# Shared buffers for the up and down stage, a paired token order in the out projection, and operand addresses equal modulo 512 bytes

## The chip, the core and the metric

The kernel runs on one core of a Trainium2 chip. Its time is the device time of one execution in microseconds (us); where several runs are given, their median. TensorE (PE) multiplies matrices into PSUM, VectorE (DVE) and ScalarE (ACT) do elementwise work, GpSimd (POOL) some more of it, and SyncE (SP) issues the DMAs, in the order in which they are written for it. A weight load of PE is listed as PEld.

## The reference

One encoder block on x of 1024 tokens by 1024 channels, in float32:

```
h = rmsnorm(x) * norm_mix_g ; proj = h @ w_in            # 1024 x 2048
u, q, k, v = split(proj, 512 columns each)
a = per group of 128 channels: (centred mean over 2, 4, 8 or 16 tokens - u) @ w_pool, times pool_scale
b = neighbourhood attention over a 16 x 64 grid, 8 heads of 64, window 8 x 16, with a relative bias
x = x + concat(a, b) @ w_out                             # 1024 x 1024
h = rmsnorm(x) * norm_mlp_g
x = x + square(relu(h @ w_up)) @ w_down                  # 1024 x 4096, 4096 x 1024
out = rmsnorm(x) * final_g
```

## The kernel before

**Split operands.** Each float32 operand is cut into a rounded high part and the remainder, both of type float32r: `split` is an ACT cast (line 90) and a DVE subtraction (line 91). `three` (lines 133, 135, 137) multiplies high by high, high by low and low by high into one PSUM bank of 128 x 512, so every product of a 128-deep slice is three wide matmuls.

**Stages.** First come the projections (operands hh and hl against weights wh, wl, wvh, wvl), the pool groups and the attention, with the projections as filler between the attention tiles (`filler`, `pump`). `out_pools` multiplies the pooled half of the mixed channels (`mixed`, split into `msp` tiles) with the first half of w_out (`woh`, `wol`) and stores the sum with x in DRAM (`ad`). The out stage (lines 748 to 768) takes the eight token tiles of 128 in order 0 to 7: it adds the attention half of w_out to the loaded `acc`, stores it as x2, normalises it into `hn2`, and one tile later `h2t` transposes it (line 724).

**Up and down stage.** Both MLP products use a seven-product scheme for 2 x 2 blocks. The token axis is cut in halves (tiles 0 to 3 and 4 to 7), the channels in halves too, and four operands `ops` are blocks while 5, 6, 7 and others are sums of blocks; tile t of one half and tile t + 4 of the other enter the same sum. In `h2t` of before, tiles 0 to 3 fill ops 1 and 2 and keep raw copies `b11r`, `b21r`; tiles 4 to 7 make t1 (ops 5), `t2r` and a raw copy `b22r`. Ops 6, 7, 3 and 4 are made after the last tile from these raw copies (`t_split`, `t_sum`, lines 832 to 846). The up stage runs over 16 pairs of blocks of w_up, seven products each in the order 1 5 6 2 7 3 4, each of 12 wide matmuls; `cut` makes the w_up operand `s` some five products ahead, `evacuate` empties PSUM, `stored` writes the results and their sums to DRAM (`us`), and `lazy` holds the sums back. Two pairs of blocks (`EARLY`) have their products 1 and 2 done while the last tiles are made ready.

Then all buffers of the up stage are closed, new ones opened, and the down stage runs its seven products over 16 blocks each: `load_d` brings two blocks of w_down and `us`, `cut_pair` splits two operands into `st` (four blocks ahead), `four` multiplies for four token tiles into four banks, `after` empties them. In the last product the last five blocks (`STAGGERED`) are held back and then done token tile by token tile, so that the closing norm of one tile runs under the matmuls of the next.

**Buffers.** Tiles come from pools with a fixed number of slots; an instruction that fills a slot waits until its former content was used up. Up to the early products the order of the work is the planner's (it simulates the program), behind them (`manual_schedule`) it is the order written. `t4` tiles of 4 KB per partition serve x, weights, mixed, msp, acc, hn2 and the early w_up operands alike, 16 slots of 4160 bytes, since the wide `t4w` shares them. `t16` has four slots for hh, hl and later w_out.

Of the kernel before, what the change touches and what calls it, by code (L numbers as in the profile page):

```python
# [30 lines left out]
NPAIR = 16  # L31
EARLY = 2


@with_exitstack
def block_kernel(ctx, tc, x, norm_mix_g, w_in, w_pool, pool_scale, rpb, w_out,
# [32 lines left out]
    def t16(name):  # L69
        return k16.tile([P, 4096], F32R, tag="k16", name=name)  # L70
# [109 lines left out]
    hh = quads([t16("hh0"), t16("hh1")])  # L180
    hl = quads([t16("hl0"), t16("hl1")])
    with ExitStack() as pv:
# [24 lines left out]
        for i in range(4):  # L207
            raw = t4("wvraw").rearrange("p (c n) -> p c n", c=2)
# [191 lines left out]
    with ExitStack() as pt_:  # L400
# [157 lines left out]
        def wo_half(i):  # L558

            wos[i] = t16("woh"), t16("wol")  # L560
            for c in range(4):
                wo_chunk(i, c)
# [15 lines left out]
        def m_split(src, th, pool, tag, eng=None):  # L578

            m = pool.tile([P, 1024], F32R, tag=tag, name="msp").rearrange("p (l t) -> p l t", l=2)  # L580
            split(m[:, 0, :], m[:, 1, :], src[:, th * HALF:(th + 1) * HALF], lo_eng=eng)
            return m

# [3 lines left out]
        def out_pools():  # L587
            wos[1] = t16("woh"), t16("wol")
            for th in range(2):
                for tt in range(4 * th, 4 * th + 4):  # L590
# [10 lines left out]
                    if th == 0:  # L601
                        later.append(lambda g=tt: ma[1].append(m_split(mixed[g], 1, qk, "qk")))
                    elif tt < 7:
                        later.append(lambda h=tt - 4: mb[0].append(m_split(bs[h], 0, k4, "k4")))
# [3 lines left out]
        def filler():  # L608

            finish = None  # L610
            for o in order[1:]:
# [11 lines left out]
                if o == "q3":  # L623
                    later.extend(lambda g=g: ma[0].append(m_split(mixed[g], 0, k4, "k4")) for g in range(4))
# [53 lines left out]
        mb[0].append(m_split(bs[3], 0, k4, "k4"))  # L678
# [7 lines left out]
    hbs = ExitStack()  # L686
    hb = hbs.enter_context(tc.tile_pool(name="hb", bufs=3, reuse_waits="tile"))
    ue = hbs.enter_context(tc.tile_pool(name="ue", bufs=EARLY, reuse_waits="tile"))
    hrs = ExitStack()
    hrp = hrs.enter_context(tc.tile_pool(name="hr", bufs=4, reuse_waits="tile"))  # L690

    def t_op(pool):
        return pool.tile([P, 2, 4, HALF], F32R, tag="h", name="hop")


    ops = {i: t_op(hb) for i in (1, 2, 5)}
    b11r, b21r, t2r, b22r = [hrp.tile([P, 4, HALF], F32, tag="hr", name="hr") for _ in range(4)]

    def load_early(b):
        raw = t4("uraw").rearrange("p (c n) -> p c n", c=NC8)  # L700
        nc.sync.dma_start(out=raw, in_=w_up[:, 2 * b * P:(2 * b + 1) * P]
                          .rearrange("(c p) n -> p c n", p=P))
        out = []
# [11 lines left out]
    def h2t(hn, tt):  # L715
# [3 lines left out]
        pts = []  # L719
        for g in range(2):  # L720
            pt = bank("ST"[g])
            for k in range(4):
                c = 4 * g + k
                nc.tensor.transpose(pt[:, k * P:(k + 1) * P], hn[:, c * P:(c + 1) * P], ident)
            pts.append(pt.rearrange("p (k t) -> p k t", k=4))
        if th == 0:
            for pv, raw, o in zip(pts, (b11r, b21r), (ops[1], ops[2])):
                nc.scalar.copy(out=raw[:, :, tsl], in_=pv)
                split(o[:, 0, :, tsl], o[:, 1, :, tsl], raw[:, :, tsl])
        else:  # L730
            t1 = t2("t1").rearrange("p (k t) -> p k t", k=4)
            nc.vector.tensor_tensor(out=t1, in0=pts[0], in1=b11r[:, :, tsl], op=ALU.subtract)
            nc.vector.tensor_tensor(out=t2r[:, :, tsl], in0=pts[1], in1=t1, op=ALU.subtract)
            nc.scalar.copy(out=b22r[:, :, tsl], in_=pts[1])
            split(ops[5][:, 0, :, tsl], ops[5][:, 1, :, tsl], t1)
# [3 lines left out]
    acc = []  # L739
    hn = None  # L740
    early = []

    def load_acc(tt):
        a = t4("acc")
        nc.sync.dma_start(out=a, in_=ad[tt * P:(tt + 1) * P, :])
        acc.append(a)
# [3 lines left out]
    for th in range(2):  # L750
        for tt in range(4 * th, 4 * th + 4):
            a = acc[tt]
            if tt + 2 < NC8:
                load_acc(tt + 2)
            for nh in range(2):
                nsl = slice(nh * HALF, (nh + 1) * HALF)
                ps = bank(("pp", "O")[tt % 2])
                run(out_half(mb[th], wos[1], tt, nh, ps))
                nc.vector.tensor_tensor(out=a[:, nsl], in0=ps, in1=a[:, nsl], op=ALU.add)
# [389 lines left out]
```

## Time and profile before

| | |
|---|---|
| median of three runs | 1043.28 us (1040.67 to 1043.54) |
| profiled execution | 1040.96 us, its span 1039.2 us |
| PE busy | 988.6 us, 95% of the span |
| DVE, ACT, POOL busy | 63%, 52%, 16% of the span |
| mean granted PE clock | 0.98 of full speed |
| DMA | 159.14 MB, mean 153 GB/s |

Busy shares are averages over stages with different limits. PE's matmuls overlap, so the duration of one is longer than the distance between two starts. Times inside the rows below count from the start of the span.

### The profile page before, as it was taken

The page shows a single profiled execution, that of the slowest core. Times are in us where ns is not written, and L with a number is a line of the kernel's source. Part 1 is how long each engine was busy: PE and PEld are TensorE (multiplying, and loading weights), DVE is VectorE, ACT ScalarE, POOL GpSimd, SP SyncE. Part 2 cuts the span into 40 slices and gives each one's busy share as a digit, 9 for nine tenths or more (in the row PEclk, how much of TensorE's full clock was granted, in tenths as well). Part 3 has the DMA queues.
Part 4 walks back from the last instruction along what each step waited for, and adds up shares of the span by engine and source line. Part 5 has one row for each costly group of instructions (what it writes and reads, how often), then busy time and mean ns, then how long its engine had stood idle before and what let it go on. Part 6 is the DMA issues. An engine that isn't in the chain of part 4 may idle for free.

```text
span 1039.2 us, 13197 instructions
## 1 busy us (share of the span) xinstructions
PE 988.6 (95%) x4508; PEld 811.8 (78%) x4508; DVE 656.5 (63%) x1149; ACT 536.6 (52%) x1037; POOL 163.1 (16%) x228
## 2 busy tenths in 40 slices
PE   8998999998999995999999999995999999999996
PEld 5786888887788883788888888884888888888884
DVE  6512677677674688676666666644577755857775
ACT  6413657566552544655655555544444554445443
POOL 3613446152440110000000000000020210002012
PEclk9999999999899998999999999997999999999998
DMA  8575333506654570464454454227966434464132
GB/s 288 159 228 123 76 86 90 139 21 144 208 202 142 181 225 20 155 200 150 131 180 134 136 178 132 102 92 273 362 216 212 142 112 137 157 203 142 41 108 95
DMA packets 102501, 159.14 MB, mean 153 GB/s; under 512 B 9377, under 2 KB 47777, under 8 KB 102434
## 3 DMA queue, kind: packets, MB, share of 16 engines
q1 hardware_dynamic: 101856, 157.25, 47.7%
q10 hardware_dynamic: 578, 1.05, 0.3%
q8 instruction: 35, 0.57, 0.2%
q14 instruction: 32, 0.26, 0.1%
HBM read 105.04 MB, written 48.79 MB: 148 GB/s over the span
## 4 chain that ended last, share of the span: by engine, by line
PE 79%; DVE 5%; DMA 4%; ACT 4%; issue 3%; SPq 3%; POOL 2%; POOLq 0%; ACTq 0%; DVEq 0%
PE ps_pp L135 12%; PE ps_pp L133 12%; PE ps_pp L137 12%; PE ps_S L137 5%; PE ps_S L133 5%; PE ps_S L135 5%; PE ps_O L137 4%; PE ps_O L133 4%; PE ps_O L135 4%; PE ps_T L133 3%; PE ps_T L137 3%; PE ps_T L135 3%; PE ps_O L539 2%; PE ps_T L526 2%; DMA vraw<-vd 1%
## 5 line engine op out<-in xcount | busy, mean ns | idle before, releaser
L91 DVE TENSOR_TENSOR st<-ur,st 128x512 fp32r<-128x512 f32 x112 | 80.1, 715 | 87.9 <-ACT st L90 87.7
L90 ACT CAST st<-ur 128x512 fp32r<-128x512 f32 x112 | 69.5, 620 | 114.1 <-PE ps_T L137 79.9
L1017 POOL TENSOR_TENSOR m<-m,x2t 128x512 f32<-128x512 f32 x16 | 23.0, 1455 | 543.7 <-ACT m L1022 533.9
L91 DVE TENSOR_TENSOR s<-wraw,s 128x512 fp32r<-128x512 f32 x76 | 52.5, 691 | 81.8 <-ACT s L90 81.8
L90 ACT CAST st<-pq 128x512 fp32r<-128x512 f32 x112 | 69.2, 618 | 41.9 <-DVE pq L1000 41.9
L133 PE MATMUL ps_pp<-hop,s 128*128 128x512 f32 x184 | 74.1, 403 | 14.2 <-ACT m L856 11.2
L91 DVE TENSOR_TENSOR st<-pq,st 128x512 fp32r<-128x512 f32 x112 | 80.1, 715 | 3.3
L869 ACT ACTIVATE r<-r 128x512 f32<-128x512 f32 x64 | 40.5, 632 | 78.1 <-DVE r L868 54.9
L133 PE MATMUL ps_pp<-hh,wh 128*128 128x512 f32 x192 | 77.1, 402 | 1.7 <-DVE q L459 1.7
L137 PE MATMUL ps_pp<-hh,wl 128*128 128x512 f32 x192 | 76.7, 400 | 0.0
L135 PE MATMUL ps_pp<-hl,wh 128*128 128x512 f32 x192 | 76.6, 399 | 0.0
L135 PE MATMUL ps_pp<-hop,s 128*128 128x512 f32 x184 | 73.8, 401 | 0.0
L137 PE MATMUL ps_pp<-hop,s 128*128 128x512 f32 x184 | 73.5, 399 | 0.0
L519 POOL TENSOR_SCALAR s<-s,ri 128x288 f32<-128x288 f32 (+1 forms) x64 | 41.8, 654 | 108.0 <-DVE ri L518 86.1
L133 PE MATMUL ps_pp<-st 128*128 128x512 f32 x112 | 44.6, 398 | 13.4 <-ACT st L90 13.4
L133 PEld LDWEIGHTS ps_pp<-hop,s 128*128 128x128 f32 x184 | 35.4, 192 | 23.6 <-ACT m L856 12.1
L515 ACT ACTIVATE s<-s,mn 128x288 f32<-128x288 f32 (+1 forms) x64 | 36.8, 576 | 27.5 <-DVE mn L503 27.0
L133 PE MATMUL ps_S<-hop,s 128*128 128x512 f32 x128 | 50.3, 393 | 0.0
L135 PE MATMUL ps_S<-hop,s 128*128 128x512 f32 x128 | 50.2, 393 | 0.0
L137 PE MATMUL ps_S<-hop,s 128*128 128x512 f32 x128 | 50.2, 393 | 0.0
L90 ACT CAST s<-wraw 128x512 fp32r<-128x512 f32 x76 | 46.2, 608 | 4.9 <-DVE wraw L820 3.6
L91 DVE TENSOR_TENSOR pth<-ps_T,pth 96x384 fp32r<-96x384 f32 (+1 forms) x64 | 35.1, 551 | 19.6 <-ACT pth L90 19.0
(225 smaller groups left out, 2691.3 us busy)
## 6 DMA issues: line engine op xcount, KB each, us to landing
ur<-us SPq DMA_DIRECT2D x56, 512.0 KB
wraw<-in_w_up_dram SPq DMA_DIRECT2D x16, 1024.0 KB
us<-r SPq DMA_DIRECT2D x64, 256.0 KB
pq<-in_w_down_dram SPq DMA_DIRECT2D x32, 512.0 KB
us<-s SPq DMA_DIRECT2D x48, 256.0 KB
xt<-in_x_dram SPq DMA_DIRECT2D x15, 512.0 KB
wraw<-in_w_in_dram SPq DMA_DIRECT2D x12, 512.0 KB
woraw<-in_w_out_dram SPq DMA_DIRECT2D x8, 512.0 KB
```

The source lines that it names most:

```text
L90: nc.scalar.copy(out=hi, in_=src)
L91: (lo_eng or nc.vector).tensor_tensor(out=lo, in0=src, in1=r32(hi), op=ALU.subtract)
L133: nc.tensor.matmul(ps, wh, ah, start=first, stop=False, skip_group_check=more)
L135: nc.tensor.matmul(ps, wh, al, start=False, stop=False, skip_group_check=more)
L137: nc.tensor.matmul(ps, wl, ah, start=False, stop=last, skip_group_check=more)
L515: nc.scalar.activation(out=s[:, :n], in_=s[:, :n], func=AF.Exp, bias=mn, scale=-1.0, accum_out=sm)
L519: nc.gpsimd.tensor_scalar(out=s[:, :n], in0=s[:, :n], scalar1=ri, scalar2=1.0, op0=ALU.mult, op1=ALU.mult)
L526: nc.tensor.transpose(pt[:4 * w, c * P:(c + 1) * P], s[:, c * 4 * w:(c + 1) * 4 * w], ident)
L539: nc.tensor.matmul(po[:, 256 * rb:256 * rb + 256], vhls[hp, j][:4 * w, c + rb, 2 * e:2 * e + 2, :], pth[:4 * w, c, :, :], start=(c == 0), ...
L869: nc.scalar.activation(out=r, in_=r, func=AF.Relu)
L1017: nc.gpsimd.tensor_tensor(out=c[tt], in0=c[tt], in1=x, op=ALU.add)
```

## The change

The narrow 4 KB tiles and the wide tiles get slots of their own (13 and 3), wide ones of 4608 bytes; two pads move the start of the pools. The operands of the up stage, seven tiles, are all allocated ahead: five in `hb`, two in `ka`, which held hh, hl and w_out before. The out stage takes the token tiles in the order 0 4 1 5 2 3 6 7, and `h2t` makes all five operands of a pair for the tile that completes it; for the last tile the second half of that is done behind four cuts. Up and down stage use the same pools: the results `tu`, the raw tiles `wr`, the split tiles `sp_` (10 slots, 12 before) and, for quarters of w_down, the tiles of the up operands. The first ten `load_d` and three `cut_pair` are issued in the last six and the last three products of the up stage. Four blocks are held back at the end instead of five, and the last norm's sum of squares is added on DVE instead of POOL. The arithmetic of the result is the same.

```diff
+NARROW, WIDE = 13, 3
+LOADS, CUTS, STAGGERED = 10, 4, 4
...
+    pad0 = ctx.enter_context(tc.tile_pool(name="pad0", bufs=1))
+    pad0.tile([P, 88], F32, name="padding0")
...
+    pad1 = ctx.enter_context(tc.tile_pool(name="pad1", bufs=1))
+    pad1.tile([P, 80], F32, name="padding1")
+    ka = ctx.enter_context(tc.tile_pool(name="ka", bufs=2, side="right", reuse_waits="tile"))
+    k2 = ctx.enter_context(tc.tile_pool(name="k2", bufs=4, side="right"))
     first = ExitStack()
-    k2 = first.enter_context(tc.tile_pool(name="k2", bufs=4, side="right"))
-    k4 = first.enter_context(tc.tile_pool(name="k4", bufs=16, side="right"))
-    k16 = first.enter_context(tc.tile_pool(name="k16", bufs=4, side="right"))
+    kb = first.enter_context(tc.tile_pool(name="kb", bufs=2, side="right"))
+    k4 = first.enter_context(tc.tile_pool(name="k4", bufs=1, side="right"))
...
-        return k4.tile([P, 1024], dt, tag="k4", name=name)
-
-    def t4w(name):
-        return k4.tile([P, 1040], F32, tag="k4", name=name)
...
+        return k4.tile([P, 1024], dt, tag="k4", name=name, bufs=NARROW)
+
+    def t4w(name, n=1040):
+        return k4.tile([P, 1152], F32, tag="k4w", name=name, bufs=WIDE)[:, :n]
...
+    hb = ctx.enter_context(tc.tile_pool(name="hb", bufs=5, reuse_waits="tile"))
...
+    ops = {i: t_op(hb) for i in (1, 5, 2, 3, 4)}
+    ops.update({i: t_op(ka) for i in (6, 7)})
...
+    def op_split(i, tsl, src):
+        split(ops[i][:, 0, :, tsl], ops[i][:, 1, :, tsl], src)
+
+    halves = {}
+
+    def h2t(hn, tt, parts=(0, 1)):
 
         th, t0 = divmod(tt, 4)
         tsl = slice(t0 * P, (t0 + 1) * P)
...
+            if th == 0:
+                halves[t0] = []
+                both = t4("both") if t0 == 2 else None
+                for g, (i, pv) in enumerate(zip((1, 2), pts)):
+                    b = t2("b") if both is None else both[:, g * HALF:(g + 1) * HALF]
+                    b = b.rearrange("p (k t) -> p k t", k=4)
+                    nc.scalar.copy(out=b, in_=pv)
+                    op_split(i, tsl, b)
+                    halves[t0].append(b)
+                return
+            tt1, tt2 = [t2("t").rearrange("p (k t) -> p k t", k=4) for _ in range(2)]
+            nc.vector.tensor_tensor(out=tt1, in0=pts[0], in1=halves[t0][0], op=ALU.subtract)
+            op_split(5, tsl, tt1)
+            nc.vector.tensor_tensor(out=tt2, in0=pts[1], in1=tt1, op=ALU.subtract)
+            op_split(6, tsl, tt2)
+            halves[t0] += [tt2, pts[1]]
+        if 1 in parts and th == 1:
+            b11, b21, tt2, b22 = halves.pop(t0)
+            nc.vector.tensor_tensor(out=b11, in0=tt2, in1=b11, op=ALU.subtract)
+            op_split(7, tsl, b11)
+            op_split(3, tsl, b22)
+            nc.vector.tensor_tensor(out=b21, in0=tt2, in1=b21, op=ALU.subtract)
+            op_split(4, tsl, b21)
...
+    tiles_o = [0, 4, 1, 5, 2, 3, 6, 7]
...
+    for n, tt in enumerate(tiles_o):
+        a = acc[tt]
+        for nh in range(2):
+            nsl = slice(nh * HALF, (nh + 1) * HALF)
+            ps = bank(("pp", "O")[n % 2])
+            run(out_half(mb[tt // 4], wos[1], tt, nh, ps))
+            nc.vector.tensor_tensor(out=a[:, nsl], in0=ps, in1=a[:, nsl], op=ALU.add)
+        nc.sync.dma_start(out=x2[tt * P:(tt + 1) * P, :], in_=a)
+        if before:
+            h2t(*before)
+        hn = t4("hn2")
+        normed(a, [gb2], hn)
+        before = hn, tt
+        if n == 0:
+            for h in range(4):
+                m_attn(h, 1, t4("msp", F32R))
+        load_acc(n + 2)
+        if n >= NC8 - EARLY - 1 and len(raw_early) < EARLY:
+            raw_early.append(load_early(len(raw_early)))
+        if n >= NC8 - EARLY:
+            early.append(split_early(raw_early[len(early)]))
...
         if b == 0:
-            h2t(hn, NC8 - 1)
+            h2t(*before, (0,))
     first.close()
...
+    u2 = ctx.enter_context(tc.tile_pool(name="u2", bufs=16, side="right", reuse_waits="tile"))
+    wr = ctx.enter_context(tc.tile_pool(name="wr", bufs=3, side="right", reuse_waits="tile"))
+    sp_ = ctx.enter_context(tc.tile_pool(name="sp_", bufs=10, side="right", reuse_waits="tile"))
...
+    cut(0, 5)
+    cut(0, 6)
+    for b in range(EARLY):
+        m1[b] = tu("m1")
+        nc.scalar.copy(out=m1[b], in_=px[b])
+    cut(1, 5)
+    cut(1, 6)
+    h2t(*before, (1,))
...
+    qp, qq, qr = quarter(hb, hb), quarter(ka, hb), quarter(ka, hb)
...
+        left = len(seq) - 1 - n
+        if left <= 5:
+            for _ in range(2):
+                if loads:
+                    load_d(*loads.pop(0))
+        if left <= 2:
+            cut_pair(*splits.pop(0))
...
-        rs = rstd([ssq, ssq22[tt]])
+        ms = small.tile([P, 1], F32, tag="ms", name="ms")
+        nc.vector.tensor_tensor(out=ms, in0=ssq, in1=ssq22[tt], op=ALU.add)
```

## Rows read from the trace of the kernel before

**Rows 1.** The page: busy us and share of the span of each engine.

```profile
PE 988.6 (95%) x4508; PEld 811.8 (78%) x4508; DVE 656.5 (63%) x1149; ACT 536.6 (52%) x1037; POOL 163.1 (16%) x228
```

**Rows 2.** Windows: length; PE, PEld, DVE, ACT, POOL busy (instructions); granted clock; DMA share, GB/s.

```profile
240.00:280.00 40.00, 35.00 (x168) 28.41 (x167) 29.97 (x68) 24.94 (x58) 15.61 (x17) 0.91 0.79 211
...
376.90:441.50 64.60, 50.46 (x209) 40.15 (x207) 46.81 (x63) 36.42 (x59) 0.79 (x2) 0.89 0.38 119
...
706.70:724.60 17.90, 5.72 (x13) 4.09 (x13) 8.95 (x15) 7.03 (x13) 0.00 (x0) 0.62 0.86 305
...
1013.00:1039.20 26.20, 16.91 (x61) 11.45 (x59) 13.79 (x23) 9.38 (x19) 5.41 (x8) 0.86 0.25 97
```

**Rows 3.** Waits of PE: us in total, times, longest.

```profile
PE ps_pp L133 <- ACT st L90: 13.4, 4, 12.2
PE ps_pp L133 <- ACT m L856: 11.2, 2, 10.3
PE ps_pp L133 <- ACT woh L90: 3.2, 1, 3.2
PE ps_pp L133 <- ACT m L838: 2.9, 1, 2.9
```

**Rows 4.** Windows of PE alone in the up and in the down stage.

```profile
460.00:700.00 240.00, 240.00 (x1044) 1.00 0.45 142
740.00:980.00 240.00, 240.00 (x1060) 1.00 0.49 166
```

**Rows 5.** Operations of PE by form: count, busy us, mean ns of one.

```profile
L133 PE MATMUL ps_pp<-hh,wh 128*128 128x512 f32 x192 | 77.1, 402 | 1.7 <-DVE q L459 1.7
...
L133 PE MATMUL ps_S<-hop,s 128*128 128x512 f32 x128 | 50.3, 393 | 0.0
...
L135 PE MATMUL ps_T<-hop,s 128*128 128x512 f32 x64 | 24.9, 389 | 0.0
...
L135 PE MATMUL ps_O<-hop,s 128*128 128x512 f32 x56 | 22.2, 396 | 0.0
```

**Rows 6.** Operations of DVE by form, 384 to 418 us.

```profile
L91 DVE TENSOR_TENSOR hop<-hr,hop 128x1024 fp32r<-128x1024 f32 x8 | 9.4, 1222 | 0.5 <-ACT hop L90 0.5
```

**Rows 7.** Timeline of PE, 376 to 385 us.

```profile
376.92 0.40 PE L133 MATMUL ps_pp<-hop,us 128*128 128x512 f32 x1
...
383.41 0.60 PE L724 MATMUL ps_S<-ident,hn 128*128 128x128 f32 x4
...
384.20 0.48 PE L133 MATMUL ps_pp<-hop,us 128*128 128x512 f32 x1
```

**Rows 8.** Timeline of DVE at the end of its last cuts.

```profile
1017.77 0.68 DVE L1000 TENSOR_TENSOR pq<-pq 128x512 f32<-128x512 f32 x1
1018.38 0.68 DVE L91 TENSOR_TENSOR st<-ur,st 128x512 fp32r<-128x512 f32 x1
1019.14 0.69 DVE L91 TENSOR_TENSOR st<-pq,st 128x512 fp32r<-128x512 f32 x1
```

**Rows 9.** Timeline of DVE, 376 to 390 us: start, length.

```profile
380.24 1.28 DVE L117 SCALAR_TENSOR_TENSOR hn<-acc,rs,gb 128x1024 f32<-128x1024 f32 x1 [1.10 <-POOL rs L102]
```

**Rows 10.** The chain that ended last, 700 to 725 us.

```profile
712.11 5.64 DMA ur<-us
717.83 1.15 ACT st L90 x2
```

**Rows 11.** Timeline of PE: its last matmul.

```profile
1031.20 0.39 PE L137 MATMUL ps_T<-st 128*128 128x512 f32 x1
```

**Rows 12.** Timeline of POOL in the tail.

```profile
1033.38 0.79 POOL L97 TENSOR_SCALAR ms<-ssq,q 128x1 f32<-128x1 f32 x1 [2.07 <-ACT y L108]
```

**Rows 13.** The chain that ended last, 245 to 270 us.

```profile
252.94 0.70 DVE msp L91
253.66 6.82 DMA woraw<-in_w_out_dram
```

**Rows 14.** Timeline of SP, 699 to 724 us.

```profile
700.81 8.44 SPq L860 DMA_DIRECT2D us<-r  x3
```

More of the change, by code (lines that the diff above doesn't have):

```diff
@@ L623, in filler @@
                 if o == "q3":
-                    later.extend(lambda g=g: ma[0].append(m_split(mixed[g], 0, k4, "k4")) for g in range(4))
+                    later.extend(lambda g=g: ma[0].append(m_split(mixed[g], 0, t4("msp", F32R))) for g in range(4))
                     for _ in range(32):
@@ L677, in block_kernel @@
         flush()
[L678 to L690, printed above, removed]
+        m_attn(3, 0, t4("msp", F32R))
+    hb = ctx.enter_context(tc.tile_pool(name="hb", bufs=5, reuse_waits="tile"))
     def t_op(pool):
-        return pool.tile([P, 2, 4, HALF], F32R, tag="h", name="hop")
-    ops = {i: t_op(hb) for i in (1, 2, 5)}
-    b11r, b21r, t2r, b22r = [hrp.tile([P, 4, HALF], F32, tag="hr", name="hr") for _ in range(4)]
+        return pool.tile([P, 2, 4, HALF], F32R, tag="h" if pool is hb else "k16", name="hop")
+    ops = {i: t_op(hb) for i in (1, 5, 2, 3, 4)}
+    ops.update({i: t_op(ka) for i in (6, 7)})
     def load_early(b):
@@ new lines, in h2t @@
+        if 0 in parts:
+            pts = []
+            for g in range(2):
+                pt = bank("ST"[g])
+                for k in range(4):
+                    c = 4 * g + k
+                    nc.tensor.transpose(pt[:, k * P:(k + 1) * P], hn[:, c * P:(c + 1) * P], ident)
+                pts.append(pt.rearrange("p (k t) -> p k t", k=4))
+            if th == 0:
[14 more added lines that the diff above has]
+            halves[t0] += [tt2, pts[1]]
@@ L748, in block_kernel, with load_acc @@
+    before = None
+    raw_early, early = [], []
+    tiles_o = [0, 4, 1, 5, 2, 3, 6, 7]
+    def load_acc(k):
+        if k < NC8:
+            tt = tiles_o[k]
+            a = acc[tt] = t4("acc")
+            nc.sync.dma_start(out=a, in_=ad[tt * P:(tt + 1) * P, :])
     load_acc(0)
     load_acc(1)
[L750 to L759, printed above, removed]
-            nc.sync.dma_start(out=x2[tt * P:(tt + 1) * P, :], in_=a)
-            if hn is not None:
-                h2t(hn, tt - 1)
-            hn = t4("hn2")
-            normed(a, [gb2], hn)
-            if th == 0:
-                mb[1].append(m_split(bs[tt], 1, k4, "k4"))
-            if tt in (4, 5):
-                early.append(load_early(tt - 4))
+    for n, tt in enumerate(tiles_o):
[19 more added lines that the diff above has]
+            early.append(split_early(raw_early[len(early)]))
@@ L793, in block_kernel @@
         load_up(b)
-    def t_split(i, src):
-        o = ops[i] = t_op(hc)
-        for k in range(2):
-            split(o[:, 0, 2 * k:2 * k + 2], o[:, 1, 2 * k:2 * k + 2], src[:, 2 * k:2 * k + 2])
-    def t_sum(dst, x, y):
-        for k in range(2):
-            sl = slice(2 * k, 2 * k + 2)
-            nc.vector.tensor_tensor(out=dst[:, sl], in0=x[:, sl], in1=y[:, sl], op=ALU.subtract)
     cuts = {}
@@ L1001, in cut_pair @@
         out = []
-        for src in (u[:, b % 2:b % 2 + 1, :], right(b)):
-            t = st.tile([P, 2, HALF], F32R, tag="st", name="st")
+        for src in (u[:, b % 4:b % 4 + 1, :], right(b)):
+            t = sp_.tile([P, 2, HALF], F32R, tag="s", name="st")
             split(t[:, 0:1], t[:, 1:2], src)
@@ L1006, in cut_pair @@
         cut_d[i, b] = out
+    seq = [(0, 5), (0, 6), (1, 5), (1, 6), (0, 7), (0, 3), (0, 4), (1, 7), (1, 3), (1, 4)]
+    seq += [(b, i) for b in range(EARLY, NPAIR) for i in (1, 5, 6, 2, 7, 3, 4)]
+    done = set(cuts)
+    queue = [x for x in seq if x not in done]
+    loads, splits = order_d[:LOADS], order_d[:CUTS]
+    for n, x in enumerate(seq):
+        while queue and seq.index(queue[0]) <= n + 5:
+            cut(*queue.pop(0))
+        multiply(*x)
+        if n >= 1:
+            evacuate(*seq[n - 1])
+            if n == 2:
+                for b in range(EARLY):
+                    evacuate(b, 2)
+        if lazy and x[1] != 7:
+            lazy.pop(0)()
+        left = len(seq) - 1 - n
[5 more added lines that the diff above has]
+            cut_pair(*splits.pop(0))
+    evacuate(*seq[-1])
+    while lazy:
+        lazy.pop(0)()
     def four(s, t, tt, ps, first, last, more):
```

155 lines of the change are left out of this document (47 added, 108 removed).

## The prediction

> **What bounds the kernel now.** I read the page first: TensorE (PE) is busy 95% of the span, every other engine far less [rows 1]. So time can come from two places alone: the gaps in PE's stream, or the pace of the stream. For the gaps I read the windows, cut where the stages meet [rows 2]. Four of them hold nearly all of what PE loses: 240 to 280 us (the loads of w_out), 376.9 to 441.5 (out stage to up stage), 706.7 to 724.6 (up stage to down stage) and the last 26 us. PE's own waits name the releasers [rows 3]: one of 10.3 us and one of 2.9 us behind ScalarE copies of m, one of 12.2 us behind the first cast of the down stage, one of 3.2 us behind woh. For the pace I read two windows of 240 us without a gap [rows 4]: the up stage starts 1044 matmuls, one per 229.9 ns, the down stage 1060, one per 226.4 ns, at the same full clock. The operation rows say which are slow [rows 5]: with the same 128x512 shape, up products into O take 396 ns and those into T 389; the projections with hh take 402.
>
> **The change part by part.** The profiled execution took 1040.96 us (span 1039.2), 2.3 us under the median of 1043.28. Savings are summed on the execution and taken off the median.
>
> *Addresses.* In the program of before, the two pads are missing and tile sizes are not multiples of 512 bytes, so pools start anywhere: the operands ops 1, 2, 5 (left pool) lie 192 bytes past a multiple of 512, ops 3, 4, 6, 7 and the cuts s (right pools) 480, and every st of the down stage 352. Product 2 goes to O (ops 2 with s: 192 against 480, 396 ns), product 4 to T (480 against 480, 389 ns), and the down stage, all equal, has the pace of the fast one [rows 4, 5]. S, which takes one product of each sort, shows 393. So a pair whose two operands agree modulo 512 is about 7 ns faster. With the pads (352 and 320 bytes) the sizes of constants, small tiles and pads add up so that the left pools start 480 past a multiple of 512, like the right ones, and t4w is 1152 wide (9 x 512 bytes): nearly all matmul operands agree. Price: up stage 16 x 7 x 12 = 1344 matmuls at 229.9 - 226.4 = 3.5 ns, 4.7 us. Before it, hh with w (576), wv (192), w_out (384) and the early products (48) are 1200 wide matmuls, mostly unequal today; at 7 ns 8.4 us, of which I take 5.3, since that stage mixes in small matmuls with their own spacing and its PE order waits here and there for other engines. Together 10. Bounds: 4.7 (only what rows 3 prove) to 13.
> The Trainium skill speaks against this term: its page SBUF — State Buffer, section "Who interferes with whom", says that PE never waits on anyone for SBUF, and TensorE: Matmul & The Clock Gate (step 1 of "Step-by-step: what each phase is for") that loading the next weights takes no bandwidth from the running matmul. By that, where an operand lies could not matter, the term would be 0 and the sum 28 instead of 38. The 396 against 389 ns disagree with it here.
>
> *Out stage to up stage.* Today only ops 1, 2, 5 are filled tile by tile; the splits and subtractions of ops 6, 7, 3, 4 come after the last token tile, as eight VectorE (DVE) splits of 1.22 us [rows 6], four subtractions as long, and the casts between them. PE has by then only the early products. The window has 209 PE instructions [rows 2], 16 of them transposes, 193 wide matmuls: 193 x 0.2264 = 43.7 us, and two times 0.8 us for eight transposes (383.4 to 384.2, [rows 7]), 45.3 of 64.6. So 19.3 us are lost, in the two waits and in matmuls at half clock (1.2 instead of 2.4 GHz) behind them; the mean granted clock is 0.89.
> In the order 0 4 1 5 2 3 6 7 the partner of a tile comes soon, and all five sums of a pair are made at once: nine DVE operations for tiles 4 to 7 where three stood, six more for each of four tiles, at 0.6 us apart [rows 8]. For tiles 4 and 5 these 7 us lie under PE's matmuls of the out stage (24 x 0.23 = 5.6 us a tile). What is late next is the pair's end. PE starts the early products at 376.9, hn of tile 7 is done at 381.5, and the transposes of tile 7 run at 383.4 [rows 7, 9]; without stalls PE is through the early products near 389.5. DVE in that time: nine operations of tile 6 behind hn, 381.5 + 5.5 = 387.0; t, lo, t2, lo of tile 7 with two casts of 0.6 us [rows 10] between, to 390.8; then the first cut (a sum, a cast, a remainder: 0.6 + 0.6 + 0.7), 392.7. PE waits 3.2 us. The four cuts and the five remaining operations of tile 7 then run ahead of PE's four products (11 us) by nearly nothing; I put 1.2 us of wait before product 7 and 1 us for half clock. 5.4 stay of 19.3: saving 14. Bounds 5 and 18: the low end is the next paragraph, the high end a perfect overlap.
> The first three w_up loads now land in space of the narrow pool. If one of these slots holds an early operand of block 1 (two of thirteen slots against the three that the load covers, by their sizes), SP waits until PE is done with it, near 389.5, and a load that takes at least 5.6 us (one of half its size does [rows 10]) and a cast put the first cut near 397. That takes back about 8 us.
>
> *Up stage to down stage.* Today all pools close first: SP gets to the first down loads behind the last stores, they run from 712.1 to 717.8, two casts follow, and PE has waited 12.2 us since its last product [rows 2, 3, 10]; the mean granted clock of the window is 0.62. 13 wide matmuls are worth 2.9 of the window's 17.9 us: 15 lost. The change issues five pairs of loads (ten DMAs, SP needs some 0.5 us each) inside the last six products and three of the four cut_pairs inside the last three. They are queued between SP's stores of block 15 and between DVE's evacuations; who waits behind them is only the release of r buffers, with 16 of them. A product lasts 2.7 us, so the first load goes out near 693 and has landed near 700, six us before it is needed. The buffers are free: qp's halves take those of ops 1 and 5, whose last products are then over. DVE, busy 63% of the span [rows 1], has room there for six splits of 0.7 us in 8 us. 1 us stays: saving 14, bounds 10 and 15.
>
> *Tail.* With four instead of five blocks held back, 12 more matmuls run before the staggered part. DVE ends its last cut at 1019.8 and PE its last matmul at 1031.4 [rows 8, 11]: 48 matmuls stand behind that cut, then 39, 9 x 0.23 = 2 us less, and 0.7 of half clock goes. The POOL addition of 0.79 us [rows 12] before the last power moves to DVE: 0.6 less. The ring of split tiles shrinks from 12 to 10, which is still the 4 cuts ahead plus the one in use. 3 us, bounds 0 and 4.
>
> *Fewer narrow buffers.* 16 shared 4 KB tiles become 13, and 3 wide ones that lie unused after the last pool group. Near 250 us four mixed, four msp, three bt, two or three vhl, two weight tiles and woraw fill 16. The load of woraw at 253.7, 6.8 us long, starts when a split of mixed at 252.9 has given a slot back, and PE waits 3.2 us for woh [rows 3, 13]. With 13, two msp come later and the third and fourth woraw with them. Cost 3 us, bounds 0 and 10 (one more 6.8 us load in series and its split, with half clock).
>
> Sum: 10 + 14 + 14 + 3 - 3 = 38; 1043.3 - 38 = **1005 us**.
>
> **The rivals.** (a) *The first w_up load waits for an early operand.* For it: it shares slots with them, and SP's queue is in order. Against: eleven of thirteen slots are harmless. 8 us back: 1013; with the far bound of the narrow buffers 1020. (b) *Down loads still come late*, because SP stands at a store of a late r when they are due; three of them held its queue for 8.4 us there [rows 14]. Half of the 14 us is lost: 1012. (c) *Alignment does nothing*: the 7 ns would belong to the bank or the place in the order. Against it: S, with a product of each sort, lies midway. 10 us less won: 1015. The rule of the Trainium skill told above would make it so. (d) *Slower: the out projection starves for narrow slots.* If mixed keeps its four until the projection starts, at most one slot is left for woraw, and eight chunks come one by one at 6.8 us of load [rows 13] and 1.9 of two casts and the last remainder [rows 8, 10], 70 us, against some 30 us of PE work beside them: 40 lost. Today's single wait there already goes with a mean clock of 0.91 over 40 us [rows 2], 3.6 us; eight waits may cost 10. 50 lost against 41 won by the rest: 1052. It decides once the splits of mixed can't be made early; today they run at 252.9, before the projection [rows 13], because they go to another pool, which the change keeps. (e) The change does not do what it says: a pad off by 32 bytes gives (c).
>
> **How the numbers follow.** A measurement here tells 0.3%, 3 us, from no change. The forecast, all parts near their sums, 997 to 1011: 0.58. (a) 0.15, (b) 0.08, (c) 0.10, (d) 0.04; several of (a) to (c) at once, 1020 to 1043: 0.05, of which 0.02 within 0.3%. The range goes from 993 (alignment at 13, out stage at 18, no slot cost) to 1023, past the priced ends of (a) to (c). Faster 0.94, same 0.02, slower 0.04.
>
> **What would show it.** Up products into O and T with one duration, and hh pairs near 390 ns; the up and down windows with equal counts; no PE wait over 4 us between 370 and 400, none over 2 at the down stage's start, and the granted clock full there. Wrong would make it: O still slower than T; the first w_up load issued after the early products; a PE wait for woh above 6 us; SP issuing the first down load after the last up product.

## The result and the profile after

The changed kernel takes 1028.3 us (median of 4 runs, 1025.85 to 1030.95) against 1043.26 for the kernel before: ratio 0.9863, 95% interval 0.9833 to 0.9892. It is faster by 15 us, where 38 were forecast, and lies above the forecast range of 993 to 1023. Its profiled execution took 1027.62 us, span 1025.8.

The page, with the row that answers to [rows 1]:

```profile
PE 983.6 (96%) x4508; PEld 811.8 (79%) x4508; DVE 658.0 (64%) x1165; ACT 532.0 (52%) x1041; POOL 167.5 (16%) x228
```

Windows of the changed kernel, cut at the same places of the program as [rows 2], with one for the out stage; columns as there:

```profile
240.00:280.00 40.00, 32.94 (x160) 26.32 (x159) 29.91 (x75) 28.30 (x66) 15.18 (x17) 0.91 0.74 193
331.00:386.40 55.40, 51.04 (x242) 41.73 (x240) 37.30 (x55) 26.02 (x48) 8.11 (x14) 0.97 0.55 181
386.40:448.00 61.60, 51.56 (x209) 40.78 (x210) 42.58 (x67) 32.48 (x58) 1.28 (x2) 0.89 0.38 126
704.40:716.40 12.00, 12.00 (x54) 9.95 (x53) 8.22 (x15) 8.07 (x15) 0.00 (x0) 1.00 1.04 394
1000.00:1025.80 25.80, 15.60 (x62) 11.02 (x60) 15.40 (x29) 9.83 (x19) 3.66 (x4) 0.88 0.27 102
```

The fourth row is the switch from the up to the down stage: no idle PE, full clock, where 0.62 stood. The third is the one that disappoints: the same 209 PE instructions as in [rows 2] in 61.6 us instead of 64.6, still at a mean clock of 0.89, and 14 us were to go there. The waits of PE say the same, beside [rows 3]: the wait behind the cast st is gone, and the one behind a copy of m is still there.

```profile
PE ps_pp L141 <- ACT m L867: 8.1, 2, 6.4
PE ps_pp L141 <- ACT woh L98: 4.2, 1, 4.2
PE ps_pp L141 <- DVE acc L786: 2.8, 1, 2.8
...
PE ps_pp L141 <- ACT st L98: 1.1, 2, 0.6
```

The third row is new: PE waits for VectorE (DVE) in the out stage. The pace of the up stage, against [rows 4] and [rows 5]: a window of 240 us, then PE's operations by form.

```profile
465.00:705.00 240.00, 240.00 (x1060) 198.66 (x1059) 148.04 (x236) 136.77 (x239) 0.00 (x0) 1.00 0.47 148
```

```profile
L141 PE MATMUL ps_pp<-hh,wh 128*128 128x512 f32 x192 | 77.3, 402 | 1.9 <-DVE q L466 1.9
...
L141 PE MATMUL ps_T<-hop,s 128*128 128x512 f32 x64 | 24.9, 389 | 0.0
...
L141 PE MATMUL ps_O<-hop,s 128*128 128x512 f32 x56 | 21.8, 389 | 0.0
```

The up stage now has the 1060 matmuls of the down stage, and O and T have one duration.

To see where the time went, the program is cut at starts of matmuls that both kernels have (us, from PE's timeline). A pair like (3,1) names a pair of blocks of w_up and the product. "Block 3" is product (3,1) of the up stage; "last up product" is the start of its last matmul; "61st down" is the 61st matmul of the down stage.

| | out stage starts | early products start | block 3 starts | last up product | 61st down | span |
|---|---|---|---|---|---|---|
| before | 326.5 | 376.9 | 455.4 | 706.5 | 735.5 | 1039.2 |
| changed | 330.9 | 386.4 | 461.6 | 709.0 | 722.8 | 1025.8 |
| saved in this piece | -4.4 | -5.1 | +3.3 | +3.7 | +15.2 | +0.7 |

So the up stage's pace and the switch came as forecast; the out stage lost 5 us, the start of the up stage gave 3 in place of 14, and the tail 0.7 in place of 3. Each row is one profile; how far profiles of the same code differ is said below. DVE's timeline in the out stage and behind it shows how:

```profile
338.57 1.29 DVE L786 TENSOR_TENSOR acc<-ps_pp,acc 128x512 f32<-128x512 f32 x2 [4.81 <-DMA acc<-ad]
...
348.58 1.29 DVE L786 TENSOR_TENSOR acc<-ps_pp,acc 128x512 f32<-128x512 f32 x2 [3.12 <-DMA acc<-ad]
...
390.13 1.27 DVE L125 SCALAR_TENSOR_TENSOR hn<-acc,rs,gb 128x1024 f32<-128x1024 f32 x1
...
403.18 0.69 DVE L836 TENSOR_TENSOR t<-wraw 128x512 f32<-128x512 f32 x1 [1.20 <-DMA wraw<-in_w_up_dram]
404.61 0.69 DVE L99 TENSOR_TENSOR s<-t,s 128x512 fp32r<-128x512 f32 x1 [0.74 <-ACT s L98]
405.34 0.69 DVE L839 TENSOR_TENSOR t<-t,wraw 128x512 f32<-128x512 f32 x1
406.77 0.69 DVE L99 TENSOR_TENSOR s<-t,s 128x512 fp32r<-128x512 f32 x1 [0.74 <-ACT s L98]
```

The kernel before has rows of the same two kinds, DVE's first sums and a cut's remainder:

```profile
337.06 1.29 DVE L759 TENSOR_TENSOR acc<-ps_pp,acc 128x512 f32<-128x512 f32 x2 [4.95 <-PE ps_pp L137]
...
406.50 0.69 DVE L91 TENSOR_TENSOR s<-wraw,s 128x512 fp32r<-128x512 f32 x1 [0.68 <-ACT s L90]
```

Three things are to be seen. DVE stands for 4.8 and 3.1 us because acc (the sums in DRAM, reloaded per token tile) is not there; before, its first two sums waited for PE. It then works with hardly a hole from 373 to 397 us, so hn of the last tile comes at 390.1 to 391.4, not at 381.5 as forecast. And behind that each w_up cut has a hole of 0.7 us between its sum and its remainder, in which ScalarE (ACT) casts. This hole could have been read from the kernel before. PE's and SP's timelines:

```profile
386.39 0.50 PE L141 MATMUL ps_pp<-hop,us 128*128 128x512 f32 x1 [1.57 <-ACT hop L98]
...
404.63 0.50 PE L141 MATMUL ps_S<-hop,s 128*128 128x512 f32 x1 [0.81 <-ACT s L98]
...
422.50 0.80 PE L141 MATMUL ps_pp<-hop,s 128*128 128x512 f32 x1 [6.43 <-ACT m L867]
```

```profile
397.54 2.17 SPq L820 DMA_DIRECT2D wraw<-in_w_up_dram  x3
```

The first w_up load leaves at 397.5, behind slots that early operands and hn hold: rival (a) took place, but DVE waits only 1.2 us for it, being late itself.

### The profile page after: what moved, and what is told of

It is laid out like the page before. It is cut to its first block, busy times and chain, and to the rows that moved or that the text cites. A ratio compares the mean times of both kernels' runs of the same rounds, so it can differ in the third digit from the quotient of the medians.

```text
span 1025.8 us, 13220 instructions
## 1 busy us (share of the span) xinstructions
PE 983.6 (96%) x4508; PEld 811.8 (79%) x4508; DVE 658.0 (64%) x1165; ACT 532.0 (52%) x1041; POOL 167.5 (16%) x228
## 4 chain that ended last, share of the span: by engine, by line
PE 76%; DMA 6%; DVE 5%; ACT 4%; SPq 3%; issue 3%; POOL 2%; ACTq 0%; POOLq 0%; DVEq 0%
PE ps_pp L143 12%; PE ps_pp L141 12%; PE ps_pp L145 12%; PE ps_S L143 5%; PE ps_S L145 5%; PE ps_S L141 5%; PE ps_O L143 4%; PE ps_O L141 4%; PE ps_O L145 4%; PE ps_T L143 3%; PE ps_T L141 3%; PE ps_T L145 3%; PE ps_O L546 2%; PE ps_T L533 2%; DMA wraw<-in_w_in_dram 2%
## 5 line engine op out<-in xcount | busy, mean ns | idle before, releaser
L99 DVE TENSOR_TENSOR st<-ur,st 128x512 fp32r<-128x512 f32 x112 | 84.5, 755 | 81.5 <-ACT st L98 81.5
L141 PE MATMUL ps_pp<-hop,s 128*128 128x512 f32 x184 | 72.6, 395 | 8.1 <-ACT m L867 8.1
L143 PE MATMUL ps_pp<-hop,s 128*128 128x512 f32 x184 | 72.2, 392 | 0.0
L145 PE MATMUL ps_pp<-hop,s 128*128 128x512 f32 x184 | 72.1, 392 | 0.0
L141 PE MATMUL ps_pp<-woh,msp 128*128 128x512 f32 x96 | 40.1, 420 | 7.0 <-ACT woh L98 4.2
L993 DVE TENSOR_TENSOR pq<-pq 128x512 f32<-128x512 f32 x64 | 46.0, 718 | 0.0
```

What stands on the lines that cost most here:

```text
L99: (lo_eng or nc.vector).tensor_tensor(out=lo, in0=src, in1=r32(hi), op=ALU.subtract)
L141: nc.tensor.matmul(ps, wh, ah, start=first, stop=False, skip_group_check=more)
L143: nc.tensor.matmul(ps, wh, al, start=False, stop=False, skip_group_check=more)
L145: nc.tensor.matmul(ps, wl, ah, start=False, stop=last, skip_group_check=more)
L993: nc.vector.tensor_tensor(out=dst(b), in0=x(b), in1=y(b), op=ALU.subtract)
```

## The experiments

All times are medians. The kernel before ran beside each group of runs, and the ratios are against it: 1043.22 us beside noalign, accwide, accahead and swap, 1041.54 beside m16, outwide, odd4 and late, 1041.82 beside pipe, combo3, combopipe and stag5, 1043.48 beside ring10, accpipe and accpipeswap. Medians of different groups can therefore differ by 2 us for no reason of the edit. Where it matters, a gain is taken from the kernel before of its own group; the changed kernel's is 15.0.

Theories for the missing 23 us: narrow slots starve the out stage; ACT's queue holds up one copy; the cuts' latency; addresses in the early stage bring nothing; the tail's ring is too small.

**acc in the wide slots (accwide), and loaded earlier as well (accahead).**

```
-            a = acc[tt] = t4("acc")
+            a = acc[tt] = t4w("acc", 1024)
```

accahead also moves `load_acc(n + 2)` ahead of the matmuls of tile n.

> The changed kernel with the acc tiles of the out stage in the three wide slots, which lie unused there; the order of the loads is kept. Theory A (the out stage starves for narrow slots: the loads of acc wait for one, VectorE stands still for 4.8 and 3.1 us near 338 and 348 us and what it did not do there is what it is late with at 386): both idle stretches go, the early products start 4 to 8 us earlier than 386.4, the time falls by 4 to 9 us. Theory B (the loads come late because they stand behind the norm in the order, slots or not): the idle stretches stay within 1 us, the time stays within 2 us. Theory C (VectorE's work per pair of tiles is simply more than PE's): idle stretches go, the early products start less than 2 us earlier.

> As the kernel with acc in the wide slots, and the load of acc two tiles on is issued ahead of the matmuls again, as before the change. Theory A (slots): about as the one with the wide slots alone. Theory B (order): the gain of 4 to 9 us comes only here. Theory C (VectorE is overloaded near the end of the out stage): no idle stretch over 1.5 us of VectorE between 332 and 362 us, and still a start of the early products later than 384 us.

Measured: accwide 1019.65 us (ratio 0.9786, 0.9761 to 0.9810), accahead 1019.74 (0.9786, 0.9763 to 0.9808). DVE's first two sums now wait for PE, as this row of accwide's timeline shows (2.6 of the 4.8 us stay as that wait), and PE reaches the early products at 381.25:

```profile
335.43 1.29 DVE L786 TENSOR_TENSOR acc<-ps_pp,acc 128x512 f32<-128x512 f32 x2 [2.58 <-PE ps_pp L145]
```

The slots were the cause, 8.6 us in the medians; the place of the load in the order was not. From the start of the out stage to block 3 accwide takes 123.6 us; the four profiles whose code there is the changed kernel's, or differs from it in where the w_up blocks lie alone (changed, late, stag5, swap), take 127.0 to 130.7, mean 128.9. The granted clock of the out stage is back at 1.00:

```profile
330.00:381.25 51.25, 49.45 (x242) 40.82 (x240) 38.23 (x56) 25.32 (x48) 8.34 (x14) 1.00 0.50 165
```

**w_up blocks over w_out's buffers (swap).** The pool wr is opened before u2 in place of after it.

> The changed kernel with two pools of the up stage exchanged: the w_up blocks lie over the buffers of w_out, the u tiles over the narrow ones. Theory (rival a of the forecast: the first load of w_up waits for slots that the early operands and the last hn hold): SP issues the first load by 388 us in place of 397.5, VectorE no longer waits for it before the first cut (1.2 us today, since VectorE is late itself), and the first cut is done 1 to 3 us earlier; the time falls by 1 to 3 us. Rival (the load is hidden anyway, VectorE's own order sets the first cut): the load is early, PE's wait before product (0,7) stays at 6 us and the time within 1 us of the changed kernel.

Measured: 1025.2 us (0.9831, 0.9809 to 0.9853). SP issues the load at 382.65, and DVE's wait for it is gone; PE's wait before (0,7) is 6.43 us as before. From the start of the out stage to block 3 it takes 128.9 us against 130.7, no more than kernels with equal code there differ (127.0 and 128.9 in late and stag5 below). Of its 3 us in the median little is sure, since the two intervals overlap. So rival (a) costs no more than DVE's 1.2 us of wait here, not 8.

**The copy of m16 earlier (m16).**

```
-        while queue and seq.index(queue[0]) <= n + 5:
+        while queue and seq.index(queue[0]) <= n + (2 if n < 3 else 5):
```

> The changed kernel with the cuts of w_up run at most 2 products ahead, not 5, during the first three products of the up stage, so that ScalarE reaches the copies m5 and m16 before the casts of (0,3), (0,4) and (1,7). Theory (PE's wait of 6.4 us before product (0,7) is the copy of m16, queued on ScalarE behind three casts that wait for VectorE, while the bank was full at 410.9): the wait falls to 2 to 3 us, that is to the cut (0,7) itself, and 3 to 4 us go. Rival (VectorE's serial work on the cuts is what PE waits for, the copy only comes last): the wait of 6.4 us is split into others of 5 us and more in sum before (0,7), (0,3) and (0,4), the first product of block 2 starts within 1 us of 440.6 and the time stays.

Measured: 1028.57 us (0.9880, 0.9859 to 0.9900). My theory fell. PE's timeline:

```profile
416.17 0.50 PE L141 MATMUL ps_pp<-hop,s 128*128 128x512 f32 x1 [1.88 <-ACT m L867]
...
446.10 0.79 PE L141 MATMUL ps_pp<-hop,s 128*128 128x512 f32 x1 [6.10 <-ACT m L867]
```

The wait before (0,7) fell from 6.4 to 1.9 us, and one of 6.1 us came 30 us later. Block 2 starts 6 us earlier (434.4 against 440.6), which neither text expected, but block 3 at 462.6, 1 us later. The copy is where a late chain shows itself, and moving it moves the place alone.

**The remainder one place later (pipe).** Each cut puts its sum on DVE and its cast on ACT; its remainder follows behind the next cut's sum. The first four cuts run in the order (0,5) (1,5) (0,6) (1,6).

```
-        split(s[:, 0], s[:, 1], src)
+        nc.scalar.copy(out=s[:, 0], in_=src)
...
+        def rest():
+            nc.vector.tensor_tensor(out=s[:, 1], in0=src, in1=r32(s[:, 0]), op=ALU.subtract)
...
+    def piped(b, i):
+        if i == 6:
+            settle()
+        rest = cut(b, i)
+        settle()
+        pending.append(rest)
```

> The changed kernel with the remainder of each w_up cut put behind the next cut's sum on VectorE, and the first four cuts in the order (0,5) (1,5) (0,6) (1,6), so that VectorE doesn't stand for 0.7 us while ScalarE casts. Theory (the latency of the chain sum, cast, remainder sets the pace of PE from 403 to 455 us; the wait on the copy of m16 is only where it shows): VectorE's idle pieces of 0.68 to 0.74 us between 403 and 425 go, the first product of block 3 starts 3 to 6 us earlier than 461.6, the time falls by as much. Rival (VectorE's work, not its waits, is too much there): block 3 starts within 1.5 us of 461.6.

Measured: 1020.88 us (0.9804, 0.9791 to 0.9818), 7.4 us better than the changed kernel in the medians and 6.0 against the kernels before of their groups (20.9 less 15.0). From the start of the out stage to block 3 it takes 123.0 us, the mean without the edit being 128.9. Block 3 starts 10 us earlier, at 451.55, of which 2.4 were there at the start of the out stage already. The window 400 to 455 of the changed kernel, then of pipe:

```profile
400.00:455.00 55.00, 46.07 (x192) 36.73 (x191) 35.81 (x57) 28.93 (x51) 0.00 (x0) 0.94 0.50 160
```

```profile
400.00:455.00 55.00, 52.21 (x218) 42.24 (x219) 41.39 (x67) 35.96 (x64) 0.00 (x0) 0.94 0.48 150
```

DVE gets 67 instructions done in place of 57, with 41.4 us of work in place of 35.8. No wait behind a copy of m over 0.6 us is left: it was the latency of sum, cast and remainder. (The new order of the first four cuts is part of this edit and was not tried alone.)

**w_out's blocks in the wide slots (outwide).** `t4("woraw")` becomes `t4w("woraw", 1024)`.

> The changed kernel with the blocks of w_out (woraw, both halves) loaded into the three wide slots, unused after the last pool group. Theory (13 narrow slots delay woraw and so the out projection: first woh matmul at 266 against 257 before, out stage at 331 against 326.5): the first load goes out before 255, the first woh matmul runs by 260, the out stage starts 3 to 5 us earlier and the time falls by 3 to 5 us, more if the narrow slots set free help acc too (then VectorE's waits of 4.8 and 3.1 us shrink). Rival (the loads stand in SP's order behind those of vraw, which wait 14 us for GpSimd's splits of v): the first load still goes out after 258 and the time stays within 2 us.

Measured: 1021.77 us (0.9815, 0.9793 to 0.9837). The first woh matmul runs at 256.2 in place of 266.0, the out stage starts at 328.3 in place of 330.9. But PE now meets the out stage before the attention is done, as its timeline shows: it waits for the split of bt. So most of the 10 us by which w_out came late were covered.

```profile
335.30 0.50 PE L141 MATMUL ps_pp<-woh,msp 128*128 128x512 f32 x1 [2.03 <-ACT msp L98]
```

**Three edits at once (combo3), and with the later remainders (combopipe).** accwide, outwide and swap together; then pipe as well.

> The changed kernel with three of the edits tried: acc and w_out's blocks in the wide slots, and the w_up blocks over w_out's buffers. If slots act at different places the gains add up: 8.6 + 6.5 + 3.1 us, 1010. If the first two cure one shortage (slots set free by the one also help the other's loads), the sum is 10 to 13 us, 1015 to 1018.

> The kernel with acc and w_out's blocks in wide slots and w_up over w_out's buffers, and the cuts with the remainder one place later. Theory (latency of the chain on VectorE and ScalarE): 3 to 6 us faster than without the last edit. Rival (VectorE's work): within 1.5 us of it.

Measured: combo3 1021.85 us (0.9810, 0.9796 to 0.9823), no better than accwide alone and slower than both forecasts, so the gains don't add: its out stage starts at 328.1, but the early products at 383.6, 55.6 us later, where accwide needs 51.3. PE waits 2.0 us for the split of bt there, as in outwide; the rest stays open. combopipe 1017.0 (0.9765, 0.9752 to 0.9778), 4.9 better: the gain of the later remainders is there too.

**accwide and pipe (accpipe), and swap with them (accpipeswap).**

> The changed kernel with acc in the wide slots and the remainder of each cut one place later. If slots and latency are two costs: the gains of 8.6 and 7.4 us add up to within 2 us, 1012 to 1014. If both give back the same backlog of VectorE: 1017 to 1019, as either alone.

> The same with the w_up blocks over w_out's buffers as well. With VectorE earlier, the first load of w_up is what the first cut waits for: theory, 1 to 4 us faster than without the exchange, SP issuing that load before 384. Rival (VectorE is still later than the load): within 1 us.

Measured: accpipe **1013.65 us** (0.9713, 0.9692 to 0.9734), accpipeswap 1014.05 (0.9717, 0.9694 to 0.9740). Slots and latency are two costs: 8.6 + 7.4 = 16 forecast, 14.7 measured in the medians; against the kernels before of their groups 8.6 + 6.0 = 14.6, and 14.9 measured. The first load, issued at 378.3 in place of 387.7, is hidden anyway. accpipe is the fastest version found. Its window from the early products on, which answers to [rows 2], has a clock of 0.97:

```profile
383.00:440.00 57.00, 53.42 (x230) 42.66 (x231) 45.37 (x72) 35.19 (x62) 1.14 (x2) 0.97 0.53 163
```

**The up stage's operands unequal again (noalign).**

```
-    pad1.tile([P, 80], F32, name="padding1")
+    pad1.tile([P, 8], F32, name="padding1")
```

> The changed kernel with the second pad 288 bytes smaller, so that the pools on the left lie 192 bytes past a multiple of 512 again, as before the change, and those on the right 480. Theory (operand addresses set the pace of the up stage alone): products that read ops 1, 5, 2, 3, 4 (now all on the left) go at 396 ns, those with ops 6 and 7 stay at 389 to 390; from product (2,6) to the last up product 3 to 6 us more than 258.6; the down stage, whose operands stay equal, unchanged; the stage before 331 us changes by less than 2 us, because its pace is not PE's stream; in all 3 to 7 us slower than the changed kernel. Rival 1 (the earlier stage gained its 5 us too and something else took it back): the out stage starts 3 to 6 us later as well, in all 8 to 12 us slower. Rival 2 (addresses do nothing, bank or order does): no form changes its duration and the time stays.

Measured: 1031.64 us (0.9896, 0.9878 to 0.9914), 3.3 slower in the median, 4.9 in the span. Its window and its forms:

```profile
465.00:705.00 240.00, 240.00 (x1036) 194.28 (x1035) 147.26 (x232) 133.97 (x230) 0.00 (x0) 1.00 0.46 142
```

```profile
L141 PE MATMUL ps_S<-hop,s 128*128 128x512 f32 x128 | 50.8, 397 | 0.7 <-ACT s L98 0.7
...
L141 PE MATMUL ps_T<-hop,s 128*128 128x512 f32 x64 | 25.3, 396 | 0.0
...
L141 PE MATMUL ps_O<-hop,s 128*128 128x512 f32 x56 | 22.2, 396 | 0.0
```

One pad, 288 bytes smaller, and T goes from 389 to 396 ns: neither the bank nor the order does it. Five of seven products are unequal here, three before, none in the changed kernel: 240 us over 1036, 1044 and 1060 matmuls are 231.7, 229.9 and 226.4 ns, which makes 7.3 (noalign) and 8.1 ns (before) for a matmul with an unequal pair.

**The early stage's operands unequal (odd4).** Narrow tiles of 1032 in place of 1024 elements, of which 1024 are used.

> The changed kernel with narrow tiles of 4128 bytes in place of 4096, so that the weights wh, wl, the msp and the early operands lie at all multiples of 32 bytes again, against hh, woh, wol and hop at 480; the operands of the up and down stage stay equal. Theory (the stage before the out stage is not paced by PE's stream, so equal addresses bring nothing there): medians of the wide pairs go back from 227 to 230 up to 233 to 235 ns, the out stage starts within 1 us of 330.9, the time stays within 2 us. Rival (the 5.3 us of the forecast were won and then lost to the narrow slots): the out stage starts 4 to 6 us later and the time rises by as much.

Measured: 1027.51 us (0.9863, 0.9843 to 0.9883). The out stage starts at 331.35 (changed: 330.9), and the time is the same. PE's form hh,wh goes from 402 to 405 ns:

```profile
L141 PE MATMUL ps_pp<-hh,wh 128*128 128x512 f32 x192 | 77.8, 405 | 2.1 <-DVE q L466 2.1
```

But it had 402 ns before the change too [rows 5], so the change did not quicken these pairs. The out projection's pairs it did: the form of woh,msp into O has 397 ns before, 392 in the changed kernel, 397 here. By these rows odd4 moves the whole early stage by 2 to 3 us (an estimate), too little for the run to tell whether PE's stream is what sets its time.

**Down loads and splits only after the last up product (late).** The lines under `left <= 5` and `left <= 2` go, and all ten loads are issued ahead of the first splits.

> The changed kernel with the first down loads and their splits issued only after the last product of the up stage, as before the change. Theory (the early issue is what took the stall of 15 us away): PE stands some 9 to 12 us behind the first cast of the down stage, a half-clock stretch behind it, 13 to 16 us slower than the changed kernel, near 1043. Rival (the shared pools, which need no closing, already do most of it): less than 8 us slower.

Measured: 1041.55 us (0.9999, 0.9985 to 1.0014), as slow as the kernel before beside it: all of the gain is gone. SP issues the first down load at 711.15; in the changed kernel it did so 12.5 us ahead of the last up matmul (708.96):

```profile
696.46 0.38 SPq L985 DMA_DIRECT2D pq<-in_w_down_dram  x1
```

PE's timeline in late:

```profile
718.45 0.80 PE L141 MATMUL ps_pp<-st 128*128 128x512 f32 x1 [11.85 <-ACT st L98]
```

From the last up product to the 61st down matmul: 29.2 us (before 29.1, changed 13.8).

**Five blocks held back (stag5), and the kernel before with ten split tiles (ring10).** `STAGGERED` is 5 in the one; in the other, `bufs=12` of the pool st becomes 10.

> The changed kernel with five blocks of the last product held back, as before the change, in place of four. Theory (the end is set by the chain of VectorE, ScalarE and GpSimd, 3.15 us a tile, since four blocks give PE only 2.7 us a tile; so the smaller number won nothing at the end): the last matmul starts 0.5 to 2 us later than with four, the span from it to the end shrinks by about 0.8 us, in all 0 to 1.5 us slower. Rival (forecast: fewer blocks are worth 2 to 2.7 us): 2 to 3 us slower.

> The kernel before with the ring of split tiles of the down stage cut from 12 to 10, nothing else. Theory (a ring of ten lets VectorE run only four blocks ahead of PE, of twelve five, so its last cut ends later and the held blocks wait longer): from the 61st down matmul to the last 1 to 2.5 us more than 295.7, VectorE's last cut about 1.3 us later, in all 1 to 2.5 us slower than before. Rival (forecast: ten are still the four cuts ahead plus the one in use, no cost): within 0.4 us in that stretch.

Measured: stag5 1026.75 us (0.9854, 0.9841 to 0.9868), which the median can't tell from the changed kernel. The profile can: from the 61st down matmul to the end 305.6 us against 303.0 in the changed kernel, and 303.0 to 304.1, mean 303.5, in all fourteen profiles with four blocks. So four blocks are worth about 2 us, as the rival said. ring10: 1044.24 us (1.0010, 0.9996 to 1.0025), again within the noise; in its profile the same piece takes 305.8 against 303.7 before. Its DVE timeline at the last cut, beside [rows 8]:

```profile
1020.34 0.69 DVE L1000 TENSOR_TENSOR pq<-pq 128x512 f32<-128x512 f32 x1
1020.94 0.69 DVE L91 TENSOR_TENSOR st<-ur,st 128x512 fp32r<-128x512 f32 x1
1021.77 0.69 DVE L91 TENSOR_TENSOR st<-pq,st 128x512 fp32r<-128x512 f32 x1
```

The last cut ends 285.6 us behind the 61st down matmul (1022.46 less 736.88) against 284.3 before (1019.83 less 735.52). DVE's lead shows where it comes from: its cuts for the 91st block are done 11.5 us before PE's first matmul on them with twelve tiles, 8.7 with ten, and for the 106th 5.6 and 4.5. DVE falls back in the last blocks, and with ten tiles it starts from one block less.

## Why the prediction was right or wrong

**Addresses, 10 forecast.** The up stage was right: from block 3 to the last up product 3.7 us, where 1092 matmuls at 3.5 ns make 3.8, and noalign takes it away again (253.2 us there, changed 247.4). (The price came from [rows 4]; the text's "rows 3" is a slip.) Rival (c) is refuted for the up stage. The Trainium skill's page "SBUF — State Buffer", section "Who interferes with whom", says that PE never waits on anyone. In the window of 465 to 705 us no row of noalign shows PE waiting either (240.00 of 240 us busy), and yet it starts 24 matmuls fewer: where its own two operands lie costs the 7 ns. The 5.3 us of the earlier stages did not come. Here the step "mostly unequal today; at 7 ns 8.4 us, of which I take 5.3" failed: its sign, hh pairs near 390 ns, stayed out (402 before and after), though the 576 pairs of hh and hl with w are nearly half of the 1200. The form of wvh with hh goes from 415 to 414 ns, that of the out projection above by 5 ns. Why the pairs with hh stayed slow, and what sets the time of that stage, was not tried.

**Out stage to up stage, 14 forecast.** From the start of the out stage to block 3 it takes 128.9 us before and 130.7 after; late and stag5, with the same code there, take 127.0 and 128.9. So nothing was won. This is the step that failed, twice over. First, "PE starts the early products at 376.9" took the out stage as unchanged: I said that DVE's nine operations for a pair lie under PE's matmuls, and counted narrow slots near 250 us alone. In the out stage acc, hn, msp and the early operands share them; acc came late, DVE stood 8 us, and what it had not done it was late with 40 us on. accwide: 8.6 us in the median, 5.3 in this piece. Second, "The four cuts and the five remaining operations of tile 7 then run ahead of PE's four products (11 us) by nearly nothing" took DVE's operations as if they ran one after the other, where each split has a hole of 0.7 us for ACT's cast; only the first cut was priced as a chain. pipe: 6.0 us, 5.8 in this piece. With both mended, accpipe goes through the piece in 116.9 us (448.66 less 331.76), 12 less than before. So the order of tiles and the sums by tile are sound; 12 of the 14 us come once slots and latency are out of the way.

**The first w_up load** waits as the sub-paragraph said (issued at 397.5), but costs about 1 us at most (swap), since DVE is later than the load.

**Up stage to down stage, 14 forecast:** 15.2 measured, and late gives it all back. Rival (b) did not take place: SP issued the first down load at 696.5, before the last up product.

**Tail, 3 forecast:** 0.7, and 0.2 by the mean of the fourteen profiles. The smaller number of held blocks is worth about 2 (stag5), near its share of the forecast; but "The ring of split tiles shrinks from 12 to 10, which is still the 4 cuts ahead plus the one in use" failed: a ring of ten alone costs 2.1 (ring10, one profile against one; the medians don't show it), since DVE enters the last blocks, in which it falls back, with 2.7 us less of a lead. The move of the addition from POOL to DVE was not tried alone.

**Fewer narrow buffers, 3 lost forecast.** Up to the start of the out stage six profiles of kernels with the same code there (changed, swap, m16, pipe, late, stag5) start it at 328.5 to 331.8, mean 330.0; the kernel before and ring10 at 326.5 and 328.4, mean 327.4: 2.6 lost, with ranges that nearly touch. That the forecast's 3 comes so near is in part luck, since the 5.3 us of the addresses, due in the same stretch, stayed out. The place was incomplete: the dearer part came in the out stage. Rival (d) had the mechanism, starving for slots, but put it at woraw, where outwide shows that cover existed: w_out 10 us earlier starts the out stage 2.6 us earlier.

## What to carry to other kernels

When buffers are cut or shared, count who holds them in every stage that draws on them, not only where they were full before; a slot that comes late stops an engine that has slack, and the bill comes where that slack was to be used. Price a chain that goes back and forth between two engines by its latency, and put the next item's first step into the hole. And a wait that names a copy may only mark where a late chain meets PE: move the copy, and see whether the time moves or only the wait.

## What the runs showed of the hardware

In the up stage a 128x512 matmul starts 226.4 ns after the one before it when both of its operands lie at the same offset from a multiple of 512 bytes, and 7 to 8 ns later when one lies at 480 and the other at 192; in noalign its duration goes from 389 to 396 ns. The offsets are worked out from the program's sizes, and only these two were compared there, so the modulus of 512 is not tested. Unexpected was that the pairs of hh with wh, meant to agree as well, stayed at 402 ns. And the same code reached the out stage between 328.5 and 331.8 us in six profiles: a difference of 3 us there means nothing, so pieces are better compared from a start inside each trace, and a gain from the kernel before that ran beside it.
